# Where the buffers of split weights lie in SBUF: two starting places or twelve

## The chip, the cores and the metric

The kernel runs on one core of a Trainium2 chip. The core has a matrix engine (TensorE, PE in the profile; the loading of its stationary operand is listed apart as PEld), a vector engine (VectorE, DVE), a scalar engine (ScalarE, ACT), GpSimd (POOL) and SyncE (SP), which here only issues DMAs. The engines work on an on-chip memory, SBUF, of 128 partitions; products are collected in PSUM. The metric is the device time of one execution in microseconds. Before the change it is 1277.83 us, the median of 2 runs (1277.57 to 1278.09).

## What is computed

A network on 256 tokens of width 1024, all in float32. First a block of two layers, each `h = h + y(rms_norm(h))`: a state space layer, then causal attention. Then two layers, each of a mixing part with three branches (latent attention, a gated convolution, retention) and a gated feed-forward part. Cut to what matters here:

```python
def first_block(x, ...):
    h = x
    for i in range(DEPTH):                      # DEPTH = 2
        hn = rms_norm(h, norm_g[i])
        y = s5_mixer(hn, ...) if i % 2 == 0 else moba_mixer(hn, ...)
        h = h + y
    return h

def moba_mixer(h, w_in, q_gain, k_gain, w_out):
    q, k, v, z = jnp.split(h @ w_in, 4, axis=-1)      # 8 heads of 128
    ...                                               # norms, rotation, causal softmax
    return (out * jax.nn.silu(z)) @ w_out
```

Nearly all the arithmetic is `x @ W` with W taken from device memory once: 334 tiles of 256 x 512 numbers and some narrower ones.

## The kernel before

**How a product is made.** Each operand in float32 is split in two parts of fewer bits, `hi` and `lo`, whose sum is the operand, and the product is the sum of three: x_hi·W_hi + x_hi·W_lo + x_lo·W_hi. `wtile` fetches a tile of weights, 2 k-blocks of 128 rows by 512 columns (512 KB, 4 KB of each partition): SP issues the DMA into a buffer `raw`; ACT rounds it into a buffer `hi` (L158); DVE forms `lo = raw - hi` (L160). Then `mm3` issues three matmuls (L165 takes hi, L166 lo, L167 hi) for each of 2 k-blocks and 2 halves of the tokens, so 12 for a tile. In them the stationary operand is a 128 x 128 block of the transposed activations (`xT` and others), loaded anew for each matmul, and the moving operand is one k-block of the tile: 512 columns, which is 2048 bytes of each partition. All 128x512 matmuls of L165 to L167 together are 4,032. There are 216 more of 256 columns and 96 of 416 from narrower tiles; in one product of the first layer (L454 and what follows it) the weights are stationary and the activations move; `gemm_raw` (L428) multiplies float32 operands that were not split.

**Who calls it.** `gemm` makes 512 columns for both halves of the tokens and then calls `pump`, which lets a piece of other work in (heads of attention, evaluation of earlier columns). `out_rows` makes the products that end a layer; the second half of the tokens runs 4 tiles behind the first. Both take their tiles from `wtile`, one after the other through the whole network.

**The buffers.** `net.stage(15, 4)` opens the first layer's stage, and `net.stage(20, 10, 0, 2)` the one in which all the rest runs. `wbuf` hands out buffers in turn: four of `raw`, and of `hi` and of `lo` four from the pool `wp`, which lives through the program; the second stage has two more of each from the stage's own pool `sp`, so there are rings of six. A pool with several buffers of a tag gives out the one that was used longest ago. A buffer can be written again when the last matmul that reads it is done; ACT's L158 waits for that.

**Where buffers begin.** A pool lays its buffers one behind the other, and what matters for the text below is the byte at which a buffer begins in its partition, modulo 2048: its *place*. All four `hi` and all four `lo` of `wp` have place 384, and the two and two of `sp` have place 1600, so the `hi` and the `lo` of one tile always have the same place, and in the second stage four tiles at 384 are followed by two at 1600. Narrow tiles (256 and 416 columns) have their second k-block at the place plus 1024 or 1664.

**The order of the work.** The order in which instructions stand on an engine is fixed when the program is built, from what depends on what and from which buffers are free at that point. At run time each engine goes through its own list and waits where something isn't ready. In the attention of the first block (`moba`), `score` (L1303, L1304) makes the scores of a head, ACT and DVE the softmax (L1306 to L1314), `turn` (L1320) transposes it, and `value` (L1331 to L1334) multiplies by the values; the transposes of the attention's output `a_o` are at L203. Around these pieces stand matmuls of weight tiles.

The lines of `wbuf` before:

```python
i = self.wn[tag] = self.wn.get(tag, -1) + 1
more = self.more.get(tag, 0)
pool, bufs = (self.wp, 4) if i % (4 + more) < 4 else (self.sp, more)
return pool.tile([128, KT, C], F32 if tag == "raw" else F32R, tag=tag, name=self.nm(tag), bufs=bufs)
```

Of the kernel before, what the change touches and what calls it, by code (L numbers as in the profile page):

```python
# [9 lines left out]
F32 = mybir.dt.float32  # L10
F32R = mybir.dt.float32r
# [4 lines left out]
PSUM = bass.MemoryType.PSUM  # L16
# [7 lines left out]
C = 512  # L24
KT = 2
# [25 lines left out]
class Net:  # L51
# [16 lines left out]
    def stage(self, pages, temps, raws=0, halves=0):  # L68
        """pages and temporaries of a stage; what an earlier stage had is given back."""
        if getattr(self, "ctx0", None):  # L70
            self.ctx0.close()
        self.ctx0 = ExitStack()
        self.temps = temps
        self.wn, self.more = {}, {"raw": raws, "hi": halves, "lo": halves}
        self.bp = self.ctx0.enter_context(self.tc.tile_pool(name=self.nm("bp"), bufs=pages))
        self.sp = self.ctx0.enter_context(self.tc.tile_pool(name=self.nm("sp"), bufs=2))
# [8 lines left out]
    def page(self, shape, name, dt=F32):  # L85
        """up to 4 KB of each partition"""
        assert int(np.prod(shape[1:])) <= 1024, shape
        return self.bp.tile(shape, dt, tag="q4", name=self.nm(name))
# [46 lines left out]
    def wbuf(self, tag):  # L135
        """buffer of a tile of weights; the stage may have some more of them"""
        i = self.wn[tag] = self.wn.get(tag, -1) + 1
        more = self.more.get(tag, 0)
        pool, bufs = (self.wp, 4) if i % (4 + more) < 4 else (self.sp, more)
        return pool.tile([128, KT, C], F32 if tag == "raw" else F32R, tag=tag, name=self.nm(tag), bufs=bufs)  # L140

# [27 lines left out]
    def gemm(self, xs, W, c0, ncols, evac, pts=None):  # L169
        """rows: out[t] = x @ W[:, c0:c0+ncols]; xs: list over k blocks of (hi, lo) aps [128, 256]."""  # L170
        KB = len(xs)
        pts = [self.acc(), self.acc()]
        for k0 in range(0, KB, KT):
            kn = min(KT, KB - k0)
            hi, lo = self.wtile(W[k0 * 128:(k0 + kn) * 128, c0:c0 + ncols], kn, ncols)
            for t in range(2):
                for k in range(kn):
                    xh, xl = xs[k0 + k]
                    s = slice(t * 128, t * 128 + 128)
                    self.mm3(pts[t][:, :ncols], xh[:, s], xl[:, s], hi[:, k, :ncols], lo[:, k, :ncols],  # L180
                             k0 + k == 0, k0 + k == KB - 1)
            self.pump()
        for t in range(2):
            evac(t, pts[t][:, :ncols])

    def split(self, dh, dl, src, scale=None):
        """dh + dl = src * scale, src in PSUM."""
# [8 lines left out]
    def transposed(self, t, row, pages, nb, gains=None, scale=None):  # L196
        """row [128 tok, nb*128] -> split blocks of pages, scaled per channel by gains."""
# [43 lines left out]
    def out_rows(self, xs, W, x, post, out=None):  # L241
        """x + rms(xs @ W) * post, or x + xs @ W when post is None; the first 128 rows are done some tiles ahead."""
        nc = self.nc
        KB = len(xs)
# [47 lines left out]
    def rsqrt1(self, v):  # L292
        """-1024 / 27 / sqrt(v) of a column, by a step of third and one of second order."""
# [16 lines left out]
    # ------------------------------------------------------------------ consts  # L310
# [25 lines left out]
    def sincos(self, out_c, out_s, ang, tag, after=None):  # L336
        """sin and cos of ang (any size that float32 reduces), ang [128, ...]"""
# [18 lines left out]
    def tables2(self):  # L356
# [8 lines left out]
        self.cs = self.sp.tile([128, 2, 2, 80], F32, tag="cs", name="cs", bufs=1)  # (cos/sin, t, mla16|ret64)  # L365
# [5 lines left out]
        # log gammas: min(x, 0) - log1p(exp(-|x|)), log1p by the atanh series  # L371
# [20 lines left out]
        # distances: [m part, mt, n]: relu(n - m), relu(m - n)  # L392
# [9 lines left out]
    # ------------------------------------------------------------------ first block: state space layer  # L402
    def raw_tiles(self, W, c0, ncols, KB):
        """sources of the tiles of gemm_raw, in its order"""
        return [W[k0 * 128:(k0 + KT) * 128, c0 + n0:c0 + n0 + C] for k0 in range(0, KB, KT) for n0 in range(0, ncols, C)]

    def load_raw(self):
        """next tile of self.todo, in any of the buffers of a tile of weights"""
# [6 lines left out]
    def gemm_raw(self, xs, ncols, evac, after=None):  # L415
        """gemm_t on float32 operands that are not split, where the tensor engine has the time: a closure for each tile of self.pre."""
# [22 lines left out]
    def gemm_t(self, xs, W, c0, ncols, evac, order=None):  # L439
        """columns: out^T = W[:, c0:c0+ncols]^T x^T, evac(block, psum [128, 256]); order of the pairs of k blocks."""  # L440
# [20 lines left out]
    def s5_params(self, after):  # L461
# [10 lines left out]
        # powers of ab: [ri, pair, k], k = 0..4  # L472
# [18 lines left out]
        # one chunk further, on (re, -im): [[a, b], [-b, a]] of ab^4  # L491
# [5 lines left out]
        # f = (ab - 1) / (lr + i li)  # L497
# [15 lines left out]
        # sums for products in three multiplications  # L513
# [4 lines left out]
    def s5_bc(self):  # L518
# [4 lines left out]
        # B~ = f B  # L523
# [20 lines left out]
    def s5_pows(self):  # L544
        """powers 1..16 of ab^4: (-im, re, im), pair, power."""
# [19 lines left out]
    def cprod(self, eng, q, l0, Z, Zx):  # L565
        """ab^l z for pairs 8q..8q+7, l = l0..l0+3, as (k1, k2, k3): re = k1 + k3, im = k1 + k2."""
# [14 lines left out]
    def s5_w(self, q, eng):  # L581
        """pairs 8q..8q+7 of ab^k B~, k = 1..4, [(g2, p), qq, (q2, k, c)], pair = 2 qq + q2, re and im."""
# [7 lines left out]
    def s5_wt(self, W, q, w, after=None):  # L590
        """their lhsT [(q2, k, c), qq, (g2, p)]"""
# [8 lines left out]
    def s5_c(self, cab, q, eng):  # L600
        """pairs 8q..8q+7 of [(g2, p), pair, (l, c')] of C ab^l, l = 0..3, re and im."""
# [4 lines left out]
    def s5(self, x_in):  # L606
# [6 lines left out]
        # normalised input; gains go on its channels after the transposes  # L613
# [6 lines left out]
        # gains go on the channels of the input; 1 / rms on what comes out of the first product and on what goes into the second  # L620
# [47 lines left out]
        # block diagonal B~ (re, -im) and the zeros before the kernel taps  # L668
# [55 lines left out]
        # chunk inputs X = W u: [(g2, p), (re, -im), pair, 1 + j], replaced by the states after each chunk  # L724
# [14 lines left out]
        # scan over the 64 chunks: inside 4 groups of 16, across the groups, then what each group takes over  # L739
# [28 lines left out]
        # kernel taps K[l] = Re(C ab^l B~): [(q4, g2, c), pg, (l, c')], channels in order; spread to lower triangles  # L768
# [19 lines left out]
        # inside a chunk  # L788
# [58 lines left out]
        # gated linear unit, output  # L847
# [25 lines left out]
    # ------------------------------------------------------------------ second block: mixing  # L873
    def mix(self, l, x):
# [11 lines left out]
        # ---- gates, branch outputs, merge  # L886
# [31 lines left out]
    def conv(self, l, xs, W, hf):  # L918
        """a * sigmoid(gate), taps, layer norm over channels and silu; the taps are left to run beside what follows."""
# [80 lines left out]
    def rope_rows(self, o1, o2, x1, x2, c, s, tag):  # L1000
        """o1 = x1 c - x2 s, o2 = x2 c + x1 s"""
# [42 lines left out]
    def mla(self, l, parts):  # L1044
        """latent attention; its rows and heads are left to run beside what follows."""
# [102 lines left out]
    def retention(self, l, xs, W, rstd, half, gn):  # L1148
# [41 lines left out]
        def score(h):  # L1190
            """scores on their decay, D^T[m, n] = gamma_f^(n - m) or gamma_b^(m - n)"""
# [54 lines left out]
    # ------------------------------------------------------------------ first block: causal attention  # L1246
# [128 lines left out]
    # ------------------------------------------------------------------ ffn  # L1375
# [25 lines left out]
def _cols(a, w):  # L1401
    """[..., w*128] -> [128, n*w]: one column per block of 128 channels."""
# [68 lines left out]
```

## Time and profile before

| | before |
|---|---|
| time of a run, median of 2 | 1277.83 us |
| span of the profiled execution | 1276.7 us |
| PE busy | 1235.7 us (97%) |
| DVE busy | 948.3 us (74%) |
| ACT busy | 652.9 us (51%) |
| DMA queue q1, share of 16 engines' span | 50.9% |
| granted TensorE clock, mean | 0.981 |

The profiled execution has no time of its own beside its span; the span is 1.1 us under the median of the runs.

How to read it: busy times of an engine are counted where one of its instructions runs. Matmuls overlap each other in the record (one is shown with 0.39 us, and the next starts 0.23 us later), so the pace of TensorE is read from the distance between starts, or from the number of PEld instructions in a stretch: each matmul has one load. A granted clock of 1.00 is full speed.

### The profile page before, as it was taken

Reading aid. Unit: us, or ns where it says so; the run is one execution under the profiler, and the core shown is the slowest. Engines: PE = TensorE matmul, PEld = TensorE weight load, DVE = VectorE, ACT = ScalarE, POOL = GpSimd, SP = SyncE. Lnnn points to the kernel's source line nnn. Section 1 sums busy time; section 2 is a strip of 40 time slices with the busy share of each in tenths; the row PEclk is TensorE's granted clock in tenths of the full one; section 3 lists DMA queues with packets and bytes.
Section 4 is the critical chain, followed back from the end, with each engine's and each line's share of the span. In section 5 each row is a group of like instructions: output and inputs, shape, how many; then the busy total and the mean of one; then the engine's idle time right before and its main releaser. Section 6 shows DMA issues by size and latency. Waiting matters only on the chain.

```text
span 1276.7 us, 17877 instructions
## 1 busy us (share of the span) xinstructions
PE 1235.7 (97%) x6520; PEld 1029.5 (81%) x6520; DVE 948.3 (74%) x1923; ACT 652.9 (51%) x1073; POOL 51.8 (4%) x42
## 2 busy tenths in 40 slices
PE   7898799999999999999999999999999999999997
PEld 6787777787888888888788887888888887888886
DVE  6999489887889998857755555899998857755544
ACT  3112467675765544544644444666545445644432
POOL 3920000000000000000000000000000000000000
PEclk9779899999999999999999999999999999999999
DMA  9326656644454554555566564544554554665661
GB/s 319 83 43 99 166 174 209 192 136 137 142 164 138 161 161 152 164 201 179 189 180 184 171 235 151 175 134 147 166 159 153 179 184 148 218 190 161 193 211 50
DMA packets 125367, 210.60 MB, mean 165 GB/s; under 512 B 22112, under 2 KB 31328, under 8 KB 125280
## 3 DMA queue, kind: packets, MB, share of 16 engines
q1 hardware_dynamic: 117056, 204.24, 50.9%
q10 hardware_dynamic: 8224, 5.23, 2.1%
q8 instruction: 51, 0.84, 0.3%
q14 instruction: 36, 0.29, 0.1%
HBM read 205.83 MB, written 3.60 MB: 164 GB/s over the span
## 4 chain that ended last, share of the span: by engine, by line
PE 79%; DVE 13%; ACT 3%; DMA 3%; issue 2%; SPq 0%; DVEq 0%; ACTq 0%
PE mm L165 23%; PE mm L167 23%; PE mm L166 22%; DVE lo L160 2%; PE sm L203 2%; ACT hi L158 1%; PE sm L1119 1%; PE sm L1211 1%; DVE cacc L957 1%; PE sm L1094 1%; DVE s5pr L745 1%; PE sm L733 1%; DVE cm L586 1%; DVE s5pr L759 1%; PE mm L455 1%
## 5 line engine op out<-in xcount | busy, mean ns | idle before, releaser
L160 DVE TENSOR_TENSOR lo<-raw,hi 128x1024 fp32r<-128x1024 f32 (+2 forms) x372 | 440.1, 1186 | 235.8 <-ACT hi L158 234.4
L158 ACT ACTIVATE hi<-raw 128x1024 fp32r<-128x1024 f32 (+2 forms) x372 | 382.6, 1032 | 377.8 <-PE mm L167 290.4
L165 PE MATMUL mm<-hi,xTh 128*128 128x512 f32 (+2 forms) x1152 | 451.1, 394 | 1.6 <-ACT xTh L193 1.5
L167 PE MATMUL mm<-hi,xTl 128*128 128x512 f32 (+2 forms) x1152 | 443.7, 386 | 0.3 <-DVE t L297 0.2
L166 PE MATMUL mm<-lo,xTh 128*128 128x512 f32 (+2 forms) x1152 | 443.3, 385 | 0.2 <-DVE lo L160 0.2
L165 PEld LDWEIGHTS mm<-hi,xTh 128*128 128x128 f32 x1152 | 216.4, 188 | 48.9 <-ACT xTh L193 7.3
L167 PEld LDWEIGHTS mm<-hi,xTl 128*128 128x128 f32 x1152 | 216.3, 188 | 46.2 <-DVE t L297 1.5
L166 PEld LDWEIGHTS mm<-lo,xTh 128*128 128x128 f32 x1152 | 216.7, 188 | 41.2 <-DVE lo L160 0.5
L957 DVE SCALAR_TENSOR_TENSOR cacc<-aT,colp,cacc 128x256 f32<-128x256 f32 x240 | 104.2, 476 | 0.0
L165 PE MATMUL mm<-hi,fh 128*128 128x512 f32 x176 | 69.0, 392 | 0.0
L166 PE MATMUL mm<-lo,fh 128*128 128x512 f32 x176 | 68.9, 392 | 0.0
L167 PE MATMUL mm<-hi,fl 128*128 128x512 f32 x176 | 68.8, 391 | 0.0
L167 PEld LDWEIGHTS mm<-hi,fl 128*128 128x128 f32 x176 | 33.0, 187 | 7.4
L165 PEld LDWEIGHTS mm<-hi,fh 128*128 128x128 f32 x176 | 33.0, 188 | 7.3
L166 PEld LDWEIGHTS mm<-lo,fh 128*128 128x128 f32 x176 | 33.0, 188 | 7.2
L277 DVE SCALAR_TENSOR_TENSOR pg<-mm,post 128x512 f32<-128x512 f32 x16 | 11.0, 690 | 21.9 <-ACT pg L275 21.9
L194 DVE SCALAR_TENSOR_TENSOR xTl<-sm,colp,xTh 128x128 fp32r<-128x128 f32 x80 | 24.3, 345 | 3.5 <-ACT xTh L193 3.1
L454 PE MATMUL mm<-s5gh,hi 128*128 128x256 f32 x64 | 19.0, 305 | 7.1 <-ACT s5gh L844 7.1
L193 ACT ACTIVATE xTh<-sm,colp 128x128 fp32r<-128x128 f32 x80 | 24.4, 381 | 1.8 <-DVE xTl L194 1.7
L895 ACT ACTIVATE pg<-mm,t 128x512 f32<-128x512 f32 x24 | 16.5, 690 | 16.9 <-PE mm L167 16.9
L733 PE MATMUL sm<-s5U,s5W 64*64 64x64 f32 x256 | 21.2, 300 | 2.5 <-DMA s5U<-s5ud 2.5
L733 PEld LDWEIGHTS sm<-s5U,s5W 64*64 64x64 f32 x256 | 20.8, 207 | 3.2 <-issue 3.2
(387 smaller groups left out, 1513.2 us busy)
## 6 DMA issues: line engine op xcount, KB each, us to landing
raw<-in_w_in SPq DMA_DIRECT2D x112, 512.0 KB, 3.5
raw<-in_ffn_w_down SPq DMA_DIRECT2D x44, 512.0 KB, 3.8
raw<-in_ffn_w_gate SPq DMA_DIRECT2D x40, 512.0 KB, 3.7
raw<-in_ffn_w_up SPq DMA_DIRECT2D x40, 512.0 KB, 3.6
raw<-in_attn_w_in SPq DMA_DIRECT2D x32, 512.0 KB, 4.3
raw<-in_ret_w_o SPq DMA_DIRECT2D x16, 512.0 KB, 3.2
raw<-in_w_out SPq DMA_DIRECT2D x16, 512.0 KB, 3.2
raw<-in_ssm_w_glu SPq DMA_DIRECT2D x8, 512.0 KB, 4.9
```

The lines of the kernel that those rows point to most:

```text
L158: nc.scalar.activation(h, r, AF.Copy)
L160: self.last_lo = nc.vector.tensor_tensor(l, r, h.bitcast(F32), op=ALU.subtract)
L165: nc.tensor.matmul(out, xh, wh, start=first, stop=False)
L166: nc.tensor.matmul(out, xh, wl, start=False, stop=False)
L167: nc.tensor.matmul(out, xl, wh, start=False, stop=last)
L193: a = nc.scalar.activation(dh, src, AF.Copy if isinstance(scale, float) else AF.Identity, scale=scale)
L194: self.last_split = a, nc.vector.scalar_tensor_tensor(dl, src, scale, dh.bitcast(F32), op0=ALU.mult, op1=ALU.subtract)
L203: nc.tensor.transpose(pt[:, b * 128:(b + 1) * 128], row[:, (b0 + b) * 128:(b0 + b + 1) * 128], self.ident)
L454: nc.tensor.matmul(o, wh, xh, start=first and b % 2 == 0, stop=False, skip_group_check=True)
L733: lx[q] = nc.tensor.matmul(pt[g * 64:g * 64 + 64, qq * 64:qq * 64 + 64], Wl[i][h][r, qq, g * 64:g * 64 + 64], U[r, 8 * h + qq, g, :], star ...
L895: nc.scalar.activation(gate[t, n], p, AF.Tanh, scale=hf(t))
L957: nc.vector.scalar_tensor_tensor(cacc[:, b, :], src, sc, cacc[:, b, :], op0=ALU.mult, op1=ALU.add)
```

## The change

`wbuf` gives each `hi` and `lo` buffer a tag of its own with one buffer, padded in front (`lead`) and behind (`tail`) by a table of numbers of 4 bytes, and picks the buffer by its index. The `raw` buffers stay as they were. Nothing is added to or taken from the arithmetic; besides the lines shown, only comments are removed, so that lines of the changed kernel have numbers higher by 7 (L158 is L165, L160 is L167, L165 to L167 are L172 to L174, L203 is L210, L1320 is L1327).

```diff
+PLACE = {"hi": ((0, 0), (0, 8), (0, 8), (0, 64), (464, 0), (288, 0)), "lo": ((4, 0), (0, 8), (0, 64), (0, 0), (288, 0), (336, 0))}
...
         i = self.wn[tag] = self.wn.get(tag, -1) + 1
         more = self.more.get(tag, 0)
-        pool, bufs = (self.wp, 4) if i % (4 + more) < 4 else (self.sp, more)
-        return pool.tile([128, KT, C], F32 if tag == "raw" else F32R, tag=tag, name=self.nm(tag), bufs=bufs)
+        i %= 4 + more
+        if tag == "raw":
+            return self.wp.tile([128, KT, C], F32, tag=tag, name=self.nm(tag), bufs=4)
+        pool = self.wp if i < 4 else self.sp
+        lead, tail = PLACE[tag][i]
+        t = pool.tile([128, lead + KT * C + tail], F32R, tag=f"{tag}{i}", name=self.nm(tag), bufs=1)
+        return t[:, lead:lead + KT * C].rearrange("p (k n) -> p k n", k=KT)
```

The places that come out of it (byte of the partition modulo 2048), with the number of 128x512 matmuls that read each buffer after the change:

| buffer | hi before | hi after | matmuls | lo before | lo after | matmuls |
|---|---|---|---|---|---|---|
| 0 | 384 | 384 | 452 | 384 | 400 | 226 |
| 1 | 384 | 416 | 444 | 384 | 448 | 222 |
| 2 | 384 | 480 | 452 | 384 | 512 | 226 |
| 3 | 384 | 768 | 452 | 384 | 1024 | 226 |
| 4 | 1600 | 0 | 448 | 1600 | 1152 | 224 |
| 5 | 1600 | 256 | 440 | 1600 | 1600 | 220 |

Pools that are opened after `wp` move with it: the pages of activations, of which the stationary operands come, by 640 bytes modulo 2048, and small temporaries from 1536 to 128.

The counters of the rings start again at 0 with each stage. The first layer uses 21 tiles, the last of them in buffer 0. Before, the first tile of the second stage got the buffer that was free longest; now it gets buffer 0 again. On ACT, at the beginning of the second stage (`hi` is written from `raw` at L158, `x` is the first layer's output, `xTh` its transpose), before:

```order
L230 ACTIVATE pg_1835,t_301_1806<-x_1632 128x512
L158 ACTIVATE hi_1902<-raw_1901 128x1024
L158 ACTIVATE hi_1920<-raw_1919 128x1024
L158 ACTIVATE hi_1938<-raw_1937 128x1024
L158 ACTIVATE hi_1956<-raw_1955 128x1024
L193 ACTIVATE xTh_1802<-sm_1807,colp 128x128
```

and after:

```order
L237 ACTIVATE pg_1835,t_301_1806<-x_1632 128x512
L165 ACTIVATE hi_1920<-raw_1919 128x1024
L165 ACTIVATE hi_1938<-raw_1937 128x1024
L165 ACTIVATE hi_1956<-raw_1955 128x1024
L165 ACTIVATE hi_1902<-raw_1901 128x1024
L200 ACTIVATE xTh_1802<-sm_1807,colp 128x128
```

The split of the first tile, hi_1902, has moved from the first to the last of the four.

On PE the two orders differ from the attention's first tiles on to the end of that layer's attention, and are the same behind it. The second four heads, before (`sm_3006` holds scores of the last head; `sm_3000`, `sm_3019` and `sm_3043` transposed softmax weights; `mm_` are products with weight tiles):

```order
L1320 MATMUL sm_3000<-first,pg_2946 128x128
L1303 MATMUL sm_3006<-akT_1887,aqT_1885 128x256
L1320 MATMUL sm_3000<-first,pg_2946 128x128 x2
L1304 MATMUL sm_3006<-akT_1887,aqT_1885 128x128
L167 MATMUL mm_3077<-hi_3140,xTl_1896 128x512
L165 MATMUL mm_3077<-hi_3140,xTh_1895 128x512
L166 MATMUL mm_3077<-lo_3141,xTh_1895 128x512
L167 MATMUL mm_3077<-hi_3140,xTl_1896 128x512
L165 MATMUL mm_3079<-hi_3140,xTh_1895 128x512
L1320 MATMUL sm_3019<-first,pg_2959 128x128
L166 MATMUL mm_3079<-lo_3141,xTh_1895 128x512
L1320 MATMUL sm_3019<-first,pg_2959 128x128 x2
```

and after:

```order
L1327 MATMUL sm_3000<-first,pg_2946 128x128
L1310 MATMUL sm_3006<-akT_1887,aqT_1885 128x256
L1327 MATMUL sm_3000<-first,pg_2946 128x128 x2
L1311 MATMUL sm_3006<-akT_1887,aqT_1885 128x128
L1327 MATMUL sm_3019<-first,pg_2959 128x128 x3
L1327 MATMUL sm_3043<-first,pg_2990 128x128 x3
L1327 MATMUL sm_3049<-first,pg_3009 128x128
L1338 MATMUL sm_3099<-rv_1888,pg_3004 128x128
L1338 MATMUL sm_3099<-rv_1888,pg_3023 128x128
L1327 MATMUL sm_3049<-first,pg_3009 128x128 x2
```

The 18 products with weights that stood between the scores of the last head and its transposes (sm_3049) now stand ahead of those scores, and nothing with weights is left between them.

The last products with weights of that stretch stood around the two transposes of the attention's output. Before (`a_o_1892` and `a_o_1893` are the two halves of the tokens):

```order
L167 MATMUL mm_3080<-hi_3166,xTl_1896 128x512
L203 MATMUL sm_3158<-first,a_o_1892 128x128 x4
L165 MATMUL mm_3080<-hi_3166,xTh_1895 128x512
L166 MATMUL mm_3080<-lo_3167,xTh_1895 128x512
L167 MATMUL mm_3080<-hi_3166,xTl_1896 128x512
L165 MATMUL mm_3077<-hi_3192,xTh_1897 128x512
L203 MATMUL sm_3184<-first,a_o_1893 128x128 x4
```

and after:

```order
L1341 MATMUL sm_3126<-rv_1889,pg_3053 128x128
L210 MATMUL sm_3158<-first,a_o_1892 128x128 x4
L172 MATMUL mm_3077<-hi_3192,xTh_1897 128x512
L210 MATMUL sm_3184<-first,a_o_1893 128x128 x4
L173 MATMUL mm_3077<-lo_3193,xTh_1897 128x512
```

Of the five products that stood there one is left, between the two transposes; the other four went ahead with the rest. The orders on SP and POOL are the same.

## Rows read from the trace of the kernel before

**Rows 1.** The page: busy time of the engines and their share of the span, the span in 40 slices (tenths) for PE and its granted clock, and the chain of work that ended last by engine and line.

```profile
PE 1235.7 (97%) x6520; PEld 1029.5 (81%) x6520; DVE 948.3 (74%) x1923; ACT 652.9 (51%) x1073; POOL 51.8 (4%) x42
PE   7898799999999999999999999999999999999997
PEclk9779899999999999999999999999999999999999
...
PE 79%; DVE 13%; ACT 3%; DMA 3%; issue 2%; SPq 0%; DVEq 0%; ACTq 0%
PE mm L165 23%; PE mm L167 23%; PE mm L166 22%; DVE lo L160 2%; PE sm L203 2%; ACT hi L158 1%; PE sm L1119 1%; PE sm L1211 1%; DVE cacc L957 1%; PE sm L1094 1%; DVE s5pr L745 1%; PE sm L733 1%; DVE cm L586 1%; DVE s5pr L759 1%; PE mm L455 1%
```

**Rows 2.** Loads of stationary operands (PEld) in eight stretches of the products that end the feed-forward parts (`out_rows`; the first five in the first of them, the last three in the second): start and end in us, length, PEld busy time (and number of loads), granted clock, DMA share, GB/s. A stretch of 24 loads is two tiles at place 1600, one of 48 four tiles at place 384.

```profile
740.12:745.73 5.60, 4.49 (x24) 1.00 0.92 332
745.73:756.62 10.90, 9.01 (x48) 1.00 0.61 209
756.62:762.23 5.60, 4.49 (x24) 1.00 0.53 187
762.23:773.12 10.90, 9.01 (x48) 1.00 0.58 195
773.12:778.73 5.60, 4.49 (x24) 1.00 0.51 152
1213.96:1224.86 10.90, 9.01 (x48) 1.00 0.74 258
1224.86:1230.46 5.60, 4.49 (x24) 1.00 0.54 189
1230.46:1241.36 10.90, 9.01 (x48) 1.00 0.57 192
```

**Rows 3.** The same columns for other stretches: the first nine 128x512 matmuls at place 384 behind an interruption, and the thirty that follow them; 24 of 256 columns at place 1600; 48 of 256 columns at place 384 (a load more than that lies on the edge of these two stretches); and four of 256 columns (L1094, attention scores) whose operands are plain float32.

```profile
313.30:315.39 2.09, 1.69 (x9) 1.00 0.54 161
315.39:322.19 6.80, 5.63 (x30) 1.00 0.25 77
728.57:731.30 2.73, 2.73 (x25) 1.00 1.02 379
1201.58:1207.32 5.74, 5.74 (x49) 1.00 0.98 358
417.75:418.61 0.86, 0.71 (x4) 1.00 0.15 55
```

**Rows 4.** The splits of the weights over the whole span, grouped by line and shape: line, engine, operation, out<-in, count, then busy time and mean ns of one, then the idle time of the engine before them and what ended it.

```profile
L160 DVE TENSOR_TENSOR lo<-raw,hi 128x1024 fp32r<-128x1024 f32 x342 | 416.8, 1222 | 205.9 <-ACT hi L158 204.6
L158 ACT ACTIVATE hi<-raw 128x1024 fp32r<-128x1024 f32 x342 | 361.6, 1061 | 344.9 <-PE mm L167 258.7 <-issue 25.3 <-DVE cacc L957 11.1
```

**Rows 5.** The timeline of ACT's splits from 743 to 755 us (start, duration; idle time before it and what ended it, in brackets); PE is on tiles at place 1600 up to 745.73 and at 384 behind.

```profile
743.12 1.06 ACT L158 ACTIVATE hi<-raw 128x1024 fp32r<-128x1024 f32 x1 [1.74 <-PE mm L167]
745.92 1.06 ACT L158 ACTIVATE hi<-raw 128x1024 fp32r<-128x1024 f32 x1 [1.74 <-PE mm L167]
748.66 1.06 ACT L158 ACTIVATE hi<-raw 128x1024 fp32r<-128x1024 f32 x1 [1.68 <-PE mm L167]
751.38 1.06 ACT L158 ACTIVATE hi<-raw 128x1024 fp32r<-128x1024 f32 x1 [1.66 <-PE mm L167]
754.11 1.06 ACT L158 ACTIVATE hi<-raw 128x1024 fp32r<-128x1024 f32 x1 [1.66 <-PE mm L167]
```

**Rows 6.** The timeline at the beginning of the second stage: the last split of ACT there, the last of DVE, and on PE the last matmul of the first layer, the transposes of its output, and the first two matmuls with weights of the second stage.

```profile
189.17 1.06 ACT L158 ACTIVATE hi<-raw 128x1024 fp32r<-128x1024 f32 x1 [0.35 <-PE mm L167]
...
189.83 1.22 DVE L160 TENSOR_TENSOR lo<-raw,hi 128x1024 fp32r<-128x1024 f32 x1
...
188.69 0.39 PE L167 MATMUL mm<-hi,s5ml 128*128 128x512 f32 x1
188.92 1.91 PE L203 MATMUL sm<-first,x 128*128 128x128 f32 x16
190.60 0.47 PE L165 MATMUL mm<-hi,xTh 128*128 128x512 f32 x1
190.91 0.39 PE L166 MATMUL mm<-lo,xTh 128*128 128x512 f32 x1
```

**Rows 7.** The second four heads of the first block's attention: the timeline of PE (scores of the last head; its first transpose; the two groups of transposes of the attention's output), of ACT (the last exponential of the last head) and of DVE (the second half of the gated output).

```profile
302.29 0.39 PE L1304 MATMUL sm<-akT,aqT 128*128 128x128 f32 x2
...
307.38 0.27 PE L1320 MATMUL sm<-first,pg 128*128 128x128 f32 x1
...
310.99 0.63 PE L203 MATMUL sm<-first,a_o 128*128 128x128 f32 x4
...
312.64 0.60 PE L203 MATMUL sm<-first,a_o 128*128 128x128 f32 x4
...
307.12 0.51 ACT L1314 ACTIVATE pg<-pg,t 128x256 f32<-128x256 f32 x1
...
311.49 0.69 DVE L1344 TENSOR_TENSOR a_o<-a_o,rg 128x512 f32<-128x512 f32 x1
```

**Rows 8.** Loads of PE for products with weights alone, from the last head's scores to its first transpose (columns as in rows 2).

```profile
302.40:307.40 5.00, 3.16 (x18) 1.00 0.29 87
```

## The prediction

> **What bounds the kernel now.** I read the page first. TensorE is busy 97% of the span, 9 tenths or more in nearly every slice after the first layer, at full granted clock; the chain that ended last runs through PE for 79%, and 68% through three lines, L165 to L167 [rows 1]. So the pace of those matmuls is the time. Then I read that pace from the loads in stretches with nothing else on PE. Two tiles at place 1600 take 5.60 us for 24 matmuls, 233.3 ns each; four tiles at place 384 take 10.90 us for 48, 227.1 ns each; the pattern repeats in both feed-forward parts [rows 2]. The DMA share is 0.92 in one of the 5.60 us stretches and 0.51 in another, so transfers don't make the difference. The load engine is busy 4.49 of 5.60 us, and where 256 columns move it is busy all the time [rows 2, 3]; so it has room with 512. What differs between the two kinds of stretch is the place of the moving operand. A second thing is to be seen: at place 384 the first nine matmuls behind an interruption take 2.09 / 9 = 232 ns, and the next thirty 6.80 / 30 = 226.7 [rows 3]. A run at one place settles into a faster pace; before it settles it runs near the pace of place 1600.
>
> **The change, part by part.** Of 4,032 matmuls of 512 columns, those of buffers 4 and 5 (448 + 440 + 224 + 220 = 1,332) stand at place 1600 before and the other 2,700 at 384; the pace is (2,700 × 227.1 + 1,332 × 233.3) / 4,032 = 229.1 ns, 924 us in all. Each ns of that mean is 4.03 us, and 2% of the time, 25.6 us, is 6.3 ns; 2% is also about what a measurement of this kernel can tell from no change.
>
> *The new places.* Afterwards 452 matmuls read from 384 and 220 from 1600; 3,360 read from places that the trace never shows. And in all six pairs hi and lo now differ, so each tile changes place with two of every three matmuls (hi, lo, hi). Only a row at one constant place shows the settled pace, so I price everything but lo's buffer 5 as unsettled: 3,812 at 232 and 220 at 233.3. Against before that is 2,700 × (232 − 227.1) = +13.2 and (1,332 − 220) × (232 − 233.3) = −1.4, +11.8 us. Some of it is paid already, because each interruption of a run at 384 costs nine matmuls at 232: about 60 products of 512 columns (334 tiles, 4 to 11 for each) are my estimate of such interruptions, 60 × 9 × 5 ns = 2.7 us. That leaves **+9 us**.
>
> Bounds: no row shows these places. From below, four matmuls of plain float32 with 256 columns take 0.86 / 4 = 215 ns [rows 3], the fastest row in which 4 bytes by about as long a stream go by; all at that pace is 4,032 × (215 − 229.1) = −57 us. From above, 48 matmuls of 256 columns at place 384 take 5.74 / 48 = 119.6 ns, so 512 columns as two such halves take 239 ns; all at that pace is +40 us. I take 232, since it is the pace of the same matmul, in the only row without a settled place, and near the middle between 215 and 239.
>
> *256 and 416 columns, and activations that move.* At 1600 24 matmuls of 256 columns take 2.73 us, 113.8 ns, at 384 119.6 [rows 3]: 216 × 6 ns is 1.3 us either way, and 96 of 416 columns less. I take 0 ± 1.5.
>
> *The splits.* DVE's L160 takes 1222 ns and ACT's L158 1061 ns [rows 4]. On ACT each waits 1.66 to 1.74 us for PE's last matmul on the old buffer before it starts, and follows the one before by 2.72 or 2.80 us with PE's pace [rows 5], so even half as long again it would stay hidden. DVE has 205.9 us before its L160 in which it waits for ACT [rows 4], 0.6 us for each. Price 0; if a new place made L160 slower by over 0.6 us where DVE is full, the cover would be gone, at up to 342 × that excess. Nothing speaks for it: both lines keep their times while the buffers change from 1600 to 384.
>
> *The ring restarts.* hi of the second stage's first tile comes last of four. The fourth split waits for the first layer's last matmul as before and ends at 189.17 + 1.06 = 190.23; now it is the first tile's, whose lo takes 1.22 more, to 191.45; PE wants that lo at 190.91 [rows 6]. +0.5 us, between 0 (if hi of this buffer is free earlier) and 2.3 (both splits, 1.06 + 1.22, on the path).
>
> *The attention's second half.* Between the last head's scores (302.29) and its transpose (307.38), which follows ACT's exponential of 307.12, PE had 18 matmuls with weights, in a stretch of 5.00 us [rows 7, 8]. They now stand ahead of the scores, so PE waits for the softmax there. 18 × 0.232 = 4.2 us of cover is lost; the softmax itself runs earlier without the splits of L158 and L160 between its steps, about 1.06 + 1.22 of the way at most, which leaves 2 to 4.2. Then the second transpose of a_o starts at 312.64, behind DVE's L1344 at 311.49 + 0.69 [rows 7], and four of the five matmuls that hid this wait are gone too: up to 4 × 0.232 = 0.9. Work done ahead of the scores may fill waits there, so the lower bound is 0, the upper 5.1. I take +3.5, nearer to the upper end, since PE shows few waits ahead.
>
> Sum: +9 + 0 + 0.5 + 3.5 = +13. The profiled span is 1276.7, the median of the runs 1277.83, 1.1 above: 1276.7 + 13 + 1.1 = **1291 us**.
>
> **The rivals.**
> *Place counts for little beyond 1600 against 384, or the settled pace survives the changes of place.* Then the mean stays at 229 and only the two order terms remain: 1277.8 + 4 = 1282 us. For it: at 1600 nothing settles lower although hi and lo share a place there, so settling is not understood. Against: behind an interruption the settled pace has to be won again [rows 3], and a change of place with every matmul may be such an interruption.
> The Trainium skill, SBUF — State Buffer, "Who interferes with whom", says "PE and ACT never wait on anyone"; ACT's rows agree (1061 ns throughout), and for PE it names no other engine, which fits the DMA shares in [rows 2], but says nothing on place.
>
> *Faster.* If most new places let a matmul of 512 columns run near the 215 ns row, the price of place is what is now paid above it, 12 to 18 ns. Halfway, at 218 to 222 ns on the mean, it is 4,032 × (220 − 229.1) = −37, +4 for the orders: about 1245 us. It decides (2%) below 229.1 − (25.6 + 4) / 4.032 = 221.8 ns. For it: 256 columns run 6 ns faster at one place than at the other, in the opposite sense to 512, so the price depends on more than the two places seen. Against: twelve places at once would have to be mostly good ones.
> The Trainium skill, TensorE: Matmul & The Clock Gate, "Back-to-back issue gap", gives N / 2.4 + 2.5 ns at full clock, 216 ns for 512 columns; [rows 2] disagree by 11 and 17 ns, and by the page all 4,032 would take 870 us, which would need the place's cost to vanish.
>
> *Slower.* If consecutive moving operands at different places, or places 400, 416 or 480 that are not multiples of 64, run at the 239 ns of two halves, the sum is +40 + 4: 1322 us. Mechanism: each of the 3,812 matmuls pays 10 ns on PE, which nothing covers. It decides above 229.1 + (25.6 − 4) / 4.032 = 234.5 ns. For it: only 2.5 ns above my price. Against: no run of 512 columns in the rows is above 233.3.
>
> **How the numbers follow.** Chances: the forecast 0.46, little effect (1282) 0.25, faster mechanism 0.14, slower mechanism 0.15. The likeliest gives 1291, its own range 1284 to 1302 (pace 231 to 234, orders 0.5 to 6). The range from 1258 to 1314 leaves out about half of each of the two outer cases. Faster by over 2% (under 1252): most of the faster case, 0.11. Slower by over 2% (over 1303.4): most of the slower case and the tail of the forecast, 0.17. Within: 0.72.
>
> **What would show it.** In the profile after: the loads of stretches like those of rows 2, tile by tile: 232 ns in each pair would bear out the forecast, a pace that goes with the buffer's place (and equal for hi's two matmuls of each three) would say that place alone counts. The splits, then L165 and L167, at 1061 and 1222 ns. At the second stage's start the second matmul waits some 0.5 us for DVE's lo. In the attention PE idles 2 to 4 us ahead of L1327 for ACT. I am wrong if a pace at a new place is below 226 or above 236 for a third of the matmuls.

## The result and the profile after

The changed kernel takes 1289.43 us, the median of 2 runs (1289.11 to 1289.76), against 1277.83 before: a ratio of 1.0092, 95% interval [1.0062, 1.0121]. It is slower by 0.9%, 11.6 us, inside the 2% that were counted as no change; 1291 was forecast.

The page of the profile after, busy times and the chain of work that ended last (to be held against [rows 1]):

```profile
span 1287.9 us, 17868 instructions
...
PE 1236.7 (96%) x6520; PEld 1025.1 (80%) x6520; DVE 945.9 (73%) x1923; ACT 653.6 (51%) x1073; POOL 42.8 (3%) x42
...
PE 73%; DVE 16%; ACT 4%; DMA 3%; issue 2%; SPq 0%; ACTq 0%; DVEq 0%
```

PE is still the bound. Its busy time is hardly longer on the whole, but that is a sum of two parts: up to 185 us, in the first layer, this execution had 150.59 us of it against 155.77 before, and behind that 1086.1 against 1079.9. The pace is read as before, from loads. One turn of the ring in the first feed-forward part of the kernel after, tile by tile; 12 loads are one tile with both halves of the tokens (in the kernel's lines the second half falls 4 tiles behind only at the end of a product, not all along). The tiles have hi and lo at places 0 and 1152, 256 and 1600, 384 and 400, 416 and 448, 480 and 512, 768 and 1024 (start and end in us, length, PEld busy time and number of loads, granted clock, DMA share, GB/s; to be held against [rows 2]):

```profile
748.21:750.95 2.75, 2.25 (x12) 1.00 0.82 286
750.95:753.73 2.77, 2.25 (x12) 1.00 0.96 342
753.73:756.51 2.78, 2.25 (x12) 1.00 0.98 348
756.51:759.30 2.79, 2.25 (x12) 1.00 0.69 228
759.30:762.10 2.80, 2.26 (x12) 1.00 0.61 191
762.10:764.83 2.73, 2.25 (x12) 1.00 0.57 200
```

For 12 matmuls that is 228.8, 231.3, 231.6, 232.5, 233.3 and 227.5 ns each (from the unrounded starts), mean 230.8. The next turn repeats each tile's length to the ns. One pair, 768 and 1024, has nearly the settled pace although its places are unequal.

The splits keep their durations, 1062 and 1223 ns against 1061 and 1222 in [rows 4]:

```profile
L167 DVE TENSOR_TENSOR lo<-raw,hi 128x1024 fp32r<-128x1024 f32 x342 | 416.8, 1223 | 212.3 <-ACT hi L165 211.1
L165 ACT ACTIVATE hi<-raw 128x1024 fp32r<-128x1024 f32 x342 | 362.2, 1062 | 353.6 <-PE mm L174 248.7 <-issue 27.1 <-DMA raw<-in_ssm_w_glu 14.4
```

The timeline of PE in the second four heads of the attention after, of its transposes L1327 and the first products behind them (idle time and what ended it, in brackets; against [rows 7]):

```profile
308.62 0.39 PE L1311 MATMUL sm<-akT,aqT 128*128 128x128 f32 x2
309.62 0.33 PE L1327 MATMUL sm<-first,pg 128*128 128x128 f32 x1 [0.61 <-ACT pg L1320]
310.11 0.71 PE L1327 MATMUL sm<-first,pg 128*128 128x128 f32 x3 [0.16 <-ACT pg L1321]
310.98 0.44 PE L1327 MATMUL sm<-first,pg 128*128 128x128 f32 x2 [0.16 <-ACT pg L1321]
313.03 0.33 PE L1327 MATMUL sm<-first,pg 128*128 128x128 f32 x1 [1.61 <-ACT pg L1320]
...
316.69 0.63 PE L210 MATMUL sm<-first,a_o 128*128 128x128 f32 x4 [0.26 <-DVE a_o L1351]
318.00 0.50 PE L172 MATMUL mm<-hi,xTh 128*128 128x512 f32 x1 [0.69 <-ACT xTh L197]
```

PE waits 0.61 + 0.16 + 0.16 + 1.61 us for the softmax and 0.26 + 0.69 around the transposes of a_o, 3.5 us in all, where it waited for none of these before.

Where the 11.2 us of the span went can be read by taking the start of the same matmul in both traces (worked out by matching the n-th 128x512 matmul of one to the n-th of the other; us):

```
start before   start after   difference   which
  185.97         185.58        -0.39      end of the first layer
  192.51         192.32        -0.20      second stage has begun
  281.89         282.20        +0.31      attention, first four heads done
  296.39         297.43        +1.04      before the second four heads
  313.31         319.02        +5.71      behind them
  608.76         616.19        +7.43      late in the first mixing part
  810.17         818.76        +8.59      behind the first feed-forward part
 1011.76        1021.34        +9.57      in the second mixing part
 1252.87        1263.99       +11.12      late in the second feed-forward part
```

The second four heads cost 4.7 us within 17. Everything else is a slow drift: 1.4 us from 185.97 to 296.39 and 5.4 us behind 313.31. There is no other step. The start of the table differs by 0.4 us already, and over all kernels here that point of the first layer comes up to 0.9 us earlier and up to 1.3 later than before; differences of two single spans are good to about 1 us.

### The profile page after: what moved, and what is told of

It is laid out like the page before. It is cut to its first block, busy times and chain, and to the rows that moved or that the text cites. A ratio compares the mean times of both kernels' runs of the same rounds, so it can differ in the third digit from the quotient of the medians.

```text
span 1287.9 us, 17868 instructions
## 1 busy us (share of the span) xinstructions
PE 1236.7 (96%) x6520; PEld 1025.1 (80%) x6520; DVE 945.9 (73%) x1923; ACT 653.6 (51%) x1073; POOL 42.8 (3%) x42
## 4 chain that ended last, share of the span: by engine, by line
PE 73%; DVE 16%; ACT 4%; DMA 3%; issue 2%; SPq 0%; ACTq 0%; DVEq 0%
PE mm L172 21%; PE mm L173 21%; PE mm L174 21%; DVE lo L167 3%; DVE cacc L964 2%; PE sm L210 2%; ACT hi L165 2%; DVE s5pr L752 1%; DMA raw<-in_attn_w_in 1%; PE sm L1126 1%; PE sm L1218 1%; PE sm L1101 1%; DVE s5X L757 1%; DMA raw<-in_w_in 1%; DVE cm L593 1%
## 5 line engine op out<-in xcount | busy, mean ns | idle before, releaser
L167 DVE TENSOR_TENSOR lo<-raw,hi 128x1024 fp32r<-128x1024 f32 (+2 forms) x372 | 440.1, 1187 | 242.9 <-ACT hi L165 241.7
L165 ACT ACTIVATE hi<-raw 128x1024 fp32r<-128x1024 f32 (+2 forms) x372 | 383.2, 1033 | 389.2 <-PE mm L174 280.9
L172 PE MATMUL mm<-hi,xTh 128*128 128x512 f32 (+2 forms) x1152 | 451.8, 394 | 2.5 <-ACT xTh L200 1.8
L174 PE MATMUL mm<-hi,xTl 128*128 128x512 f32 (+2 forms) x1152 | 444.5, 387 | 0.3
L172 PEld LDWEIGHTS mm<-hi,xTh 128*128 128x128 f32 x1152 | 216.4, 188 | 50.8 <-ACT xTh L200 6.9
L174 PEld LDWEIGHTS mm<-hi,xTl 128*128 128x128 f32 x1152 | 216.5, 188 | 47.0 <-DVE t L304 1.5
L172 PE MATMUL mm<-hi,fh 128*128 128x512 f32 x176 | 69.2, 393 | 0.0
L174 PE MATMUL mm<-hi,fl 128*128 128x512 f32 x176 | 69.1, 392 | 0.0
L172 PEld LDWEIGHTS mm<-hi,fh 128*128 128x128 f32 x176 | 33.0, 188 | 7.5
L174 PEld LDWEIGHTS mm<-hi,fl 128*128 128x128 f32 x176 | 33.0, 188 | 7.5
L435 PE MATMUL mm<-s5x,raw 128*128 128x256 f32 x96 | 22.7, 391 | 1.1 <-ACT s5x L647 1.1
L1396 ACT ACTIVATE pg<-mm,t 128x512 f32<-128x512 f32 (+1 forms) x24 | 15.6, 652 | 14.6 <-PE mm L174 14.5
```

Source lines behind the costliest of these rows:

```text
L165: nc.scalar.activation(h, r, AF.Copy)
L167: self.last_lo = nc.vector.tensor_tensor(l, r, h.bitcast(F32), op=ALU.subtract)
L172: nc.tensor.matmul(out, xh, wh, start=first, stop=False)
L174: nc.tensor.matmul(out, xl, wh, start=False, stop=last)
L435: self.last_raw = nc.tensor.matmul(o, raw[:, k, b * 128:b * 128 + 128], xs[k0 + k], start=k0 + k == 0 and b % 2 == 0, stop=k0 + k == len(x ...
```

## Experiments

**Places and order apart.** The first two kernels divide the change in two. In e1 the buffers are handed out by counters that go on through the stages, as the rings of the pools did, so that the order is that of before; the numbers of `PLACE` are rewritten so that the same twelve places come out:

```diff
         i %= 4 + more
+        k = f"{tag}{i < 4}"
+        c = self.wn[k] = (self.wn.get(k, -1) + 1) % (4 if i < 4 else more)
+        i = c if i < 4 else 4 + c
```

(`stage` keeps the counters of `wp`; the same lines are in all kernels from e3 to e10.)

> The twelve places of the change, but with the buffers handed out in the same turn as before, so that the order of the instructions on every engine is that of before (but for two matmuls that stand five rows earlier at the end of the first layer). Theory A (the changed kernel's two costs add up: about 5 us in the attention from the order, the rest from the places): about 1284.5 us, 4 to 5 us below the changed kernel's 1289.4, and no wait of PE for the softmax. Rival B (the order costs nothing, the places all): 1289. Rival C (the order costs all, the places nothing): 1278.

Measured: 1284.61 us, 1.0049 [1.0033, 1.0064], span 1282.3. No wait for the softmax is left:

```profile
engine line waited for: us in total, times, longest us
PE sm L1285 <- DVE pg L1024: 0.5, 2, 0.3
```

(all waits of PE between 185 and 340 us; L1285 is the transpose that waited for DVE before, too, there L1275). The span is 5.6 us above before and 5.6 below the changed kernel: theory A, with half for each.

e2 is the other half, the order without the padding:

```diff
-PLACE = {"hi": ((0, 0), (0, 8), (0, 8), (0, 64), (464, 0), (288, 0)), "lo": ((4, 0), (0, 8), (0, 64), (0, 0), (288, 0), (336, 0))}
+PLACE = {"hi": ((0, 0), (0, 0), (0, 0), (0, 0), (0, 0), (0, 0)), "lo": ((0, 0), (0, 0), (0, 0), (0, 0), (0, 0), (0, 0))}
```

> The order of the changed kernel (each buffer with a tag of its own, ring restarted with the stage) without padding, so that the places are those of before. Theory A (order and places add up): 1277.8 + 5 = 1283 us, with PE waiting 2 us and more for the softmax in the attention and 227 and 233 ns for a matmul as before. Rival B (places cost all): 1278. Rival C (order costs all): 1289.

Measured: 1287.54 us, 1.0068 [1.0052, 1.0084], 4.5 us above the expectation; span 1284.4: 7.7 us more than before, 2 more than the order costs in the changed kernel. Windows of PE (length, busy time, instructions, granted clock, then DMA) show why, first e2 and then the changed kernel:

```profile
308.00:312.40 4.40, 1.93 (x11) 0.91 0.34 87
312.40:318.30 5.90, 5.82 (x28) 0.50 0.07 26
318.30:320.40 2.10, 1.41 (x9) 0.98 0.17 41
```

```profile
308.00:313.00 5.00, 2.48 (x13) 1.00 0.32 81
313.00:316.70 3.70, 3.41 (x28) 1.00 0.09 34
316.70:318.70 2.00, 1.31 (x10) 1.00 0.05 20
```

Behind the same waits the granted clock was 0.50 in e2, the lower of its two levels, and the same 28 matmuls took 5.90 us instead of 3.70. In the changed kernel it stayed at 1.00. So the order's price is 5.6 us, and 2.2 more where the clock falls. What decides that wasn't tried.

**What the pace goes with.** The prediction took the place of the moving operand as what counts. But the change also moved the pages of activations, from which the stationary operands come. e3 moves them alone (lo's fourth buffer gets 640 bytes behind it, and hi's fifth enough in front of it to stay at 1600):

```diff
+PLACE = {"hi": ((0, 0), (0, 0), (0, 0), (0, 0), (352, 0), (0, 0)), "lo": ((0, 0), (0, 0), (0, 0), (0, 160), (0, 0), (0, 0))}
```

> Order and places of the moving operands as before (384 and 1600), but what lies behind those buffers, the activations that are the stationary operands among it, is moved by 640 bytes, as the change moved it (place 1024 instead of 384). Theory A (the pace goes with the place of the moving operand alone): 1278 us, 226.7 to 227 ns at 384 and 233.3 at 1600. Rival D (the pace goes with the distance between moving and stationary operand): 384 loses its settled pace and gets about the 231.4 ns that buffer 0 of hi had in the changed kernel, 2,700 x 4.3 ns = 11 us more, or less if 1600 gets faster in turn: 1280 to 1290 us.

Measured: 1283.65 us, 1.0040 [1.0025, 1.0056]. Windows of loads, two tiles at 384 and then two at 1600:

```profile
752.84:755.62 2.78, 2.26 (x12) 1.00 0.62 198
755.62:758.41 2.79, 2.26 (x12) 1.00 0.58 199
758.41:761.17 2.76, 2.25 (x12) 1.00 0.63 188
761.17:763.92 2.75, 2.25 (x12) 1.00 0.57 188
```

At place 384 a matmul now takes 231.7 to 232.6 ns instead of 227, at 1600 228.8 to 229.8 instead of 233.3 [rows 2]. The moving operands lie where they lay. Theory A of this run, the moving operand's own place, is out; what is left is how the moving operand lies to what moved, the stationary operand among it. The stationary blocks of a page lie 512 bytes apart, so I counted the distance of the two, the place of the moving one less that of the stationary one, modulo 512: before, 384 had distance 0 and 1600 distance 192; in e3 they have 384 and 64.

e4 puts all twelve at 384, with the activations where they were:

```diff
+PLACE = {"hi": ((0, 0), (0, 0), (0, 0), (0, 0), (208, 0), (0, 0)), "lo": ((0, 0), (0, 0), (0, 0), (0, 0), (0, 0), (0, 0))}
```

> Order as before, all twelve buffers at place 384, activations where they were. Theory A (each place has its pace): the 1,332 matmuls that were at 1600 go from 233.3 to 227 ns, 8.3 us less: 1269.5 us. Rival D (the distance of moving and stationary operand): the same, since the activations stay at 384 plus multiples of 512. Rival E (the two last buffers are slow for where their pool lies or for their part in the ring, not for the place): 1278 us.

Measured: 1271.98 us, 0.9949 [0.9931, 0.9967]. Rival E is out. Two tiles in a row; all others of that stretch have 2.72 us as well, 226.7 ns for a matmul:

```profile
750.11:752.83 2.72, 2.25 (x12) 1.00 0.62 200
752.83:755.55 2.72, 2.25 (x12) 1.00 0.60 191
```

e5 is e4 with everything behind the first `raw` buffers moved by 640 bytes, weights and activations together (160 words ahead of hi's first buffer):

> Order of before, all twelve buffers at place 1024 and the activations at place 1024 too: as e4, but everything moved by 640 bytes. Theory D (the pace goes with the distance of moving and stationary operand modulo 512; here 0 as in e4): 226.7 ns settled, about 1272 us as e4. Rival A (the moving operand's own place): 384 gave 232 with the activations at 1024, 1024 gave 228.5 in the changed kernel, so about 228.5 x 4,032: 1276 us and no difference where the activations lie.

Measured: 1273.40 us, 0.9960 [0.9946, 0.9974]. The 2,902 matmuls of 512 columns that stand behind at least eight of their kind have a mean of 226.8 ns: distance 0 at another place, the same pace.

e6 and e7 give each pair one place, at twelve distances in all:

```diff
+PLACE = {"hi": ((16, 0), (16, 0), (16, 0), (16, 0), (160, 0), (32, 0)), "lo": ((0, 0), (0, 0), (0, 0), (0, 64), (0, 0), (0, 0))}
...
+PLACE = {"hi": ((8, 0), (16, 0), (16, 0), (16, 0), (176, 0), (24, 0)), "lo": ((0, 0), (0, 0), (0, 0), (0, 72), (0, 0), (0, 0))}
```

> hi and lo of a pair at the same place, six places at distances 64, 128, 192, 256, 320 and 448 modulo 512 from the activations; order of before. Theory D gives 229 to 230 at 64 (place 1600 in e3), 233.3 at 192 (place 1600 before), nothing is known of the others; each pair should hold one pace through its tiles. Rival A: nothing at these places goes with the distance, 64 and 192 don't repeat the paces of e3 and before.

> As e6 with distances 32, 96, 160, 224, 384 and 480. Theory D gives 232 to 232.5 at 384 (place 384 in e3); the others lie between 226 and 236 as all seen so far. Rival A: 384 doesn't repeat its pace.

Measured: 1283.81 and 1291.07 us, one run each. Loads of one turn of the ring, first e6 (distances 192, 256, 64, 320, 448, 128), then e7 (96, 160, 224, 32, 384, 480):

```profile
750.92:753.71 2.79, 2.25 (x12) 1.00 0.71 240
753.71:756.47 2.76, 2.25 (x12) 1.00 0.59 188
756.47:759.23 2.76, 2.25 (x12) 1.00 0.58 190
759.23:761.98 2.75, 2.25 (x12) 1.00 0.62 183
761.98:764.77 2.79, 2.26 (x12) 1.00 0.64 185
764.77:767.55 2.78, 2.26 (x12) 1.00 0.62 197
```

```profile
751.42:754.23 2.81, 2.26 (x12) 1.00 0.93 303
754.23:757.03 2.80, 2.25 (x12) 1.00 0.67 216
757.03:759.84 2.80, 2.25 (x12) 1.00 0.64 205
759.84:762.64 2.80, 2.25 (x12) 1.00 0.61 192
762.64:765.44 2.80, 2.25 (x12) 1.00 0.61 189
765.44:768.24 2.80, 2.25 (x12) 1.00 0.53 188
```

No distance of the twelve reaches 226.7: they take 229 to 234 ns. 64 repeats e3 (2.76; 2.75 to 2.76 there); 192 has 2.79 where it had 2.80 before, and 384 2.80 where e3 had 2.78 to 2.79, so in these stretches, for pairs at one place, the distance gives the pace to about 1 ns, not exactly.

e8 tests the step of the prediction. All buffers have distance 0, but three pairs are unequal (384 and 896, 896 and 1408, 1920 and 384):

```diff
+PLACE = {"hi": ((0, 0), (0, 0), (0, 0), (0, 0), (208, 0), (128, 0)), "lo": ((128, 0), (0, 0), (0, 0), (0, 0), (128, 0), (128, 0))}
```

> Order of before; all buffers at distance 0 modulo 512 from the activations, but at places 384, 896, 1408 and 1920, so that hi and lo of three of six pairs have different places. Theory D: every matmul settles at 226.7, about 1272 us as e4. The step of the prediction (a pair of unequal places never settles, 232 ns): 2,010 of the matmuls at 232, 10.6 us above e4, 1282 us.

Measured: 1272.20 us, 0.9951 [0.9936, 0.9966]. Loads of four tiles: an equal pair at 896 and the three unequal ones:

```profile
748.33:751.05 2.72, 2.25 (x12) 1.00 0.63 216
751.05:753.77 2.72, 2.25 (x12) 1.00 0.53 182
753.77:756.49 2.72, 2.25 (x12) 1.00 0.62 200
756.49:759.21 2.72, 2.25 (x12) 1.00 0.62 191
```

Unequal places settle as well as equal ones.

**The stationary operand itself.** In e3 more than the stationary operands moved: buffers of ACT and DVE too. e9 and e10 leave everything of e4 where it is and read the stationary block 64 or 16 bytes further on. Both halves of the tokens then take the same 128 tokens, so these two kernels leave out the products of the others and serve for the pace alone:

```diff
-                    s = slice(t * 128, t * 128 + 128)
+                    s = slice(16, 16 + 128)
...
-            s = slice(t * 128, t * 128 + 128)
+            s = slice(16, 16 + 128)
```

> As e4 (all twelve buffers at place 384, activations at 384), but in the products with weights both halves of the tokens take tokens 16 to 143 as their stationary operand instead of 0 to 127 and 128 to 255: nothing moves in memory, only the reading of the stationary operand begins 64 bytes later, distance 448 modulo 512. The order of the instructions changes at the beginnings of stages, by some us at most. Theory D: the pace in the feed-forward stretches goes from 226.7 to the 232.4 that distance 448 had in e6, 4,032 x 5 ns = 20 us more than e4, about 1292 us. Rival F (not the stationary operand but something else that lies behind the weights counts, such as buffers of ACT and DVE): 226.7 as in e4.

> As e9, but with tokens 4 to 131 for both halves: the reading of the stationary operand begins 16 bytes later, distance 496. Nothing with a distance under 32 was seen. If the settled pace needs distance 0 exactly, some 230 to 235 ns; if it only needs to be near, 226.7.

Measured: 1304.49 us, 1.0197 [1.0182, 1.0213], and 1299.29 us in the one run of e10. Loads of a tile, e9 and then e10:

```profile
751.34:754.14 2.80, 2.26 (x12) 1.00 0.92 258
```

```profile
750.53:753.33 2.80, 2.27 (x12) 1.00 0.91 281
```

233.3 ns in both stretches, though nothing moved in memory: rival F is out. Over the whole kernel the 128x512 matmuls have 233.3 ns in e9 and 231.7 in e10, against 227.6 in e4. That is 23 us of e9's 32.5 us over e4; e9 came out 12 us above the expectation, and the rest lies in the changed order and new waits at the beginnings of stages: PE is idle 54.7 us of the span against 45.9 in e4, and between 255 and 345 us alone it waits 1.9 us more for ACT's xTh. A kernel in which both halves take the same block at distance 0 was not run; e3 lost the pace without that change.

The mean of e10 hides two paces. Loads of two tiles in each of three runs of matmuls that follow each other in e10, with all operands at distance 496 throughout:

```profile
1130.11:1135.55 5.44, 4.50 (x24) 1.00 0.60 188
1152.14:1157.74 5.60, 4.53 (x24) 1.00 0.61 175
1176.03:1181.47 5.44, 4.50 (x24) 1.00 0.55 178
```

That is 226.7, 233.3 and 226.7 ns. Each run of matmuls in e10 keeps one of the two from its first tiles to its end; of 206 groups of twelve matmuls (each behind at least eight others), 55 were at 227 and 151 at 233. In e9 all 207 such groups were at 233, in e4 all 205 at 227 to 228. So 16 bytes off the pace can be lost, but isn't always; at distance 0 the runs of e4 all have it but for their beginnings, and 64 bytes off, in e9, none has.

**Do they add up?** e11 has the places of e4 and the order of the changed kernel:

> All twelve buffers at place 384 as in e4, in the order of the changed kernel. If places and order add up: e4's 1272 plus the 5.6 us that the changed kernel has over e1, 1277.6 us; plus another 2 if the clock falls in the attention as it did in e2.

Measured: 1278.88 us (10 runs), 1.0001 [0.9991, 1.0011]; 6.9 us above e4, with the waits of the changed kernel (2.2 us for L1320 among them) and, in the profiled execution, a granted clock of 0.73 on the mean from 312.0 to 318.3 us (0.50 from 312.96 to 316.38):

```profile
308.00:312.00 4.00, 2.58 (x13) 1.00 0.15 28
312.00:318.30 6.30, 4.92 (x29) 0.73 0.19 67
```

They add up to about 1 us: e4's 1272.0 and the order's 5.6 make 1277.6, and up to 2.2 more where the clock falls. The gain of the good places and the loss of the order cancel, so this kernel is as fast as the one before.

## Why the prediction was right, and where it was right for a wrong reason

The sum came within 2 us partly by luck: the places were priced 3.4 us too high, and the order's two terms, 4 us together, were 1.6 too low against 5.6 measured.

**What bounds the kernel** was read rightly: all kernels here differ by the pace of L165 to L167 and by waits of PE, in e2 and e11 also by the clock behind such waits, and beyond about 1 us by nothing else that shows.

**The new places, +9 us.** Measured: 5.6 us (e1's span against that of before; the mean distance of two starts, over 3,764 and 3,775 neighbouring 128x512 matmuls, went from 229.7 to 231.0 ns in the changed kernel, 5.2 us for 4,032). The sign held, and the price of 232 ns roughly (230.8 in the turn above), but the step that led to it, that a pair of unequal places never settles, is wrong: unequal pairs settle in e8, and the pair 768 and 1024 nearly did in the changed kernel itself. In its place: a run settles at 226.7 ns when moving and stationary operand begin at the same offset modulo 512 bytes, as e4, e5 and e8 show, and e9, which moves the stationary reading alone by 64 bytes, never does. The change left that offset for nine of its twelve buffers, since it also moved the activations. The section on the change noted that move, and the prediction gave it no price; in the trace of before all stationary blocks begin at the same offset modulo 512, so it could not show one. The term was too high because three of the twelve (512, 1024 and 0) still have distance 0 and some others (256, 64) cost 2 to 4 ns in e3 and e6, not 5. An estimate from the tiles of e6 and e7, with about 232.5 and 233 for the distances 416 and 400 that they lack, gives 230.7 ns for the twelve distances on the mean, close to the 230.8 measured; single tiles are off by about 2 ns either way. That the price of "unsettled" fitted is luck: most other distances cost about that.

**The pace of 233.3 at 1600** was taken as a property of that place. It is one of the distance 192: with the activations moved, 1600 took 229 to 230 ns and 384 lost its pace (e3).

**Narrow tiles and splits, 0.** The splits held their durations to 1 ns. Neighbouring matmuls of 256 columns started 118.2 ns apart on the mean, 118.0 before.

**The ring restart, +0.5 us.** About 0.2 us (the table of starts, from -0.39 ahead of it to -0.20 behind). The wait that was named did not come: the lo of the first tile did come late and its matmul started 0.48 us later than before in the trace (191.39 against 190.91, [rows 6]), but that lo was done at 191.14. The build had put the next matmul with hi ahead of it, and this one waited 0.34 us, for ACT's xTh.

**The attention's second half, +3.5 us.** 4.7 us in the table of starts, of which 3.5 are the waits shown; the whole order costs 5.6 (changed kernel less e1). The waits at L1327 for the softmax, 2.5 us, are the ones named. The other 0.95 us have the size forecast, 0.9, but not the place: the second transpose of a_o did not wait; the first did, 0.26 us for DVE's a_o, and the one product left between them 0.69 us for ACT's xTh. The term came out near its upper bound, 5.1; if the work done ahead of the scores filled any wait, the sum doesn't show it, and 1.2 of the 4.7 us are not put down to a wait.

**The rivals.** "The settled pace survives the changes of place" is right as a mechanism where all distances are 0 (e8), but at nine of the twelve places of the change they are not. The faster one is out for every distance seen: nothing is under 226.7, let alone at 215. The slower one, 239 ns, was not reached by any tile; the slowest had 234.2 (distance 96).

The Trainium skill, SBUF — State Buffer, "Who interferes with whom", lists PE's read ports for the moving operand and for the load of the stationary one as independent. For the pace e9 does not bear that out: the place from which the stationary operand is read changed the pace of the same moving operands by 6.7 ns of 226.7. The measurement decides.

**What stays open.** Why distance 0 is the good one, and how 229 to 234 ns come out at the others. The distance alone doesn't settle it: operands at the same one, 496, held 226.7 in one run of e10 and 233.3 in the next, and the same two distances gave 228.8 ns in the changed kernel and 232.7 in e1 (places 0 and 1152, 12 matmuls of 2.75 and 2.79 us). Distances between 0 and 16 bytes were not tried, nor what decides between e10's two paces, nor what makes the clock fall in e2 and e11 and not in the changed kernel.

## What to carry to other kernels

When a stream of matmuls with a load for each runs some per cent over its best stretch, look at how the moving and the stationary operand lie to each other, not only at where the moving one lies; here the same offset modulo 512 bytes for all was worth 0.5% (e4 and e8, 6 to 7 us under before). That is a finding for 512 columns: matmuls of 256 columns from the weight tiles started 119.8 ns apart on the mean in e4 and e8, 118.0 before and 117.4 in e9, so for them distance 0 is the slower one, as the 119.6 and 113.8 ns of [rows 3] hinted. An edit of one pool moves the buffers of every pool behind it, so what was held constant has to be read from the addresses. And a change of tags changes in what turn buffers come free, and with it the order that the build chooses: of 11 us lost here, half came with the order, 2.5 of them as waits for a softmax that had lost its cover.

## What the runs showed that I had not expected

Sixteen bytes off distance 0, a run of matmuls has one of two paces, 226.7 or 233.3 ns, and keeps it to its end (e10); in the feed-forward stretch it was 233.3, as at 64 bytes throughout (e9). And a wait of PE has a second price that comes and goes: behind the same waits the granted clock was 0.50 over 5.9 us in e2, costing 2.2 us, 0.50 over 3.4 us in e11, and 1.00 in the changed kernel.
